# Hybrid block on Trainium2: the linear recurrence of the last two token blocks moved beside the attention's heads 5 to 7, with buffers of its own

## The chip, the cores and the metric

One Trainium2 chip, one core of it. The metric is the device time of one execution in microseconds (us); the time of a kernel is the median of its runs.

## What is computed

One layer of a hybrid encoder, f32, width 1024, on 2048 tokens with 16 learned meta tokens ahead of them (T = 2064). A normalised input goes through one projection `w_in`, whose columns are shared out among three groups of heads that do not depend on each other:

```
p = rms_norm(h, norm_mix_pre) @ w_in          # split by columns into the three groups
y = concat(rg_lru_group, forgetting_attention_group, rwkv7_group)
h = h + rms_norm(y @ w_out, norm_mix_post)
h = h + rms_norm(ffn(rms_norm(h, norm_ffn_pre)), norm_ffn_post)   # conv-gated, 2816 wide
```

The group that the change moves is the gated linear recurrence (LRU) of 256 channels:

```
u = causal_dwconv(xa, conv_w) + conv_b                  # 4 taps
r, i = sigmoid(u @ ga_w + ga_b), sigmoid(u @ gx_w + gx_b)   # 4 heads of 64x64
log_a = -8 * r * softplus(-lam);  a = exp(log_a)
b = sqrt(-expm1(2 * log_a)) * (i * u)
h_t = a_t * h_(t-1) + b_t                               # scan over the tokens
out = h * gelu(ya)
```

The attention has 8 heads of 64, causal, with a decay per token added to the scores; RWKV-7 has 4 heads of 64 with a 64x64 state that runs through the tokens.

## The kernel before

**Stages.** The input projection comes in three parts (matmuls at L193 to L195). Beside it, and on into the next stage, runs the generator `recurrences(part)`: token blocks 0 to 2, 3 to 5 and 6 to 8 (block 0 has 208 tokens, blocks 1 to 7 have 256, block 8 has 64). For each block it runs the RWKV part up to a point called SOLVED, then `R.ending`, which is what is left of the RWKV part of the block before, and then `lru_block` for the block. After the loop the rest of `R.ending` (block 8's own) is run out, the recurrences' pools are closed, and the attention follows in the program. Then come `w_out`, the feed-forward up and down products, each in three matmuls of split operands, and the output.

**Order.** Each engine executes its own instructions strictly in order. That order is not the program's: the kernel is written with generators and then laid out by a scheduler, which lets the attention's first heads run in among the last recurrences. `tc.issue_after(x)` keeps what is in it from being placed ahead of x. SyncE (SP) issues nearly all DMAs, also in order.

**The LRU** (`lru_block`, L1529 to L1591) works on two halves of 128 channels, so four chunks for blocks 7 and 8. One chunk loads its input (L1549), makes the convolution `rwlu` (ScalarE L1556, three VectorE L1558), two gate matmuls into one PSUM bank `eps` (L1563, L1564), reads that bank with ScalarE and VectorE (L1565 to L1567), goes through ScalarE and VectorE by turns (L1568 to L1580, with a square root at L1579, which loads another activation table), scans (L1581), keeps the last column as state `lru_h` (L1582), makes the gelu of the second input in `rwlr` (L1585 to L1589, a tanh at L1588), multiplies (L1590) and stores to `scr_mix` (L1591). `R.t` gives its SBUF buffers (`rwlu` two deep), `R.pe` its bank.

**RWKV closing chain.** The last pieces of a block: small matmuls into `rps` (L1316 to L1472), each read by VectorE or ScalarE before the next can go; a normalisation in VectorE on `rwgsm` and `rwxu` (L1453 to L1461, with a Newton square root at L79 to L84), and the output gate (L1472 to L1480).

**Attention** (`Attn.run`). Half 0 takes query blocks 0 and 1 of all 8 heads, half 1 query blocks 2 and 3. For each head and block `maxima` makes score tiles (L644) in the two-deep PSUM ring `at.mx`, VectorE reduces each to a maximum `mc` (L649), and four transposes (L659, the same ring) make a shift of it. Two steps (AHEAD) later `weights` makes the scores again (`sc`, L773 and L774), ScalarE's exponential (L778), sums on VectorE or GpSimd (L817), and the product with the values (`po`, L796); 14 such products for each head in half 0. `tick` is called within this and on every second call advances a generator `beside`, which is empty in half 0 and works on the 16 meta tokens in half 1. At the start of half 1 `rear` prepares a third buffer for keys, `k2_2`: its fixed rows are cast from the identity (L566), its pool taken before half 0.

Of the kernel before, what the change touches and what calls it, by code (L numbers as in the profile page):

```python
# [1 line left out]

# [6 lines left out]
F32 = mybir.dt.float32  # L9
# [9 lines left out]
P = 128  # L19
# [491 lines left out]
class Attn:  # L511
# [63 lines left out]
    def t(self, shape, tag, dt=F32, bufs=2):  # L575
        return self.pool.tile(shape, dt, tag=tag, name=self.core.n(tag), bufs=bufs)
# [335 lines left out]
    def run(self, pool, third):  # L912


        self.queue = self.nc.sync
        ready = []
        for half, bs in enumerate(((0, 1), (2, 3))):
            if half:
                self.rear(third, "k2_2")
                self.beside = self.meta(pool)  # L920
            for h in range(NH):
                self.wide = (half, h) >= WIDE
                with self.core.tc.issue_after(self.core.settled) if not half and h < 2 else nullcontext():
                    keys = self.keys(h, 4 * bs[-1] + 5)
                for b in bs:
                    gen, total, out = self.maxima(h, b, keys), self.pieces(b), []

                    def fill(share, gen=gen, total=total, out=out):
                        while len(out) < min(total, share * total):
                            out.append(next(gen))  # L930

                    if len(ready) == self.AHEAD:
                        self.weights(*ready.pop(0), fill)
                    fill(1.0)
                    ready.append((h, b, keys, next(gen)))
                    self.serial += 1
                    self.later.append((self.clock + self.FINISH, self.serial, lambda gen=gen: next(gen, None)))
                    self.later.sort(key=lambda x: x[:2])
                    if len(ready) < self.AHEAD + 1 and not half and h == 0:
                        next(gen)  # L940
        self.tail = True
        for i, step in enumerate(ready):
            if i == len(ready) - 1:
                self.queue = self.nc.gpsimd
            self.weights(*step, lambda share: None)
        self.flush()
        for _ in self.beside:
            pass
        while len(self.later) > 1:
            self.later.pop(0)[2]()  # L950
# [644 lines left out]

class Banks:


# [554 lines left out]
PACE = 1.25  # L2155

WIDE = (0, 5)

LATE, NORMS = 8, 2

# [35 lines left out]
def recurrences(core, R, lk, f_bias, scr, blocks, part):  # L2196


    for blk in blocks:
        gate_block(core, R, f_bias, scr, blk[2])  # L2200
        yield
    for b in ((0, 1, 2), (3, 4, 5), (6, 7, 8))[part]:
        gen = R.block(b)
        while next(gen) != R.SOLVED:
            yield
        yield from R.ending
        R.ending = gen
        yield from lru_block(core, R, scr, lk, b)


_INS = [
# [9 lines left out]
def hybrid_block_kernel(ctx: ExitStack, tc: tile.TileContext, args, out):  # L2221
    a = {s: v[0] if s != "meta_tokens" else v for s, v in args.items()}
    nc = tc.nc
    core = Core(tc, ctx)
    scr = scratch(tc, ctx, core)
# [8 lines left out]
    def pool(es, name, bufs, **kw):  # L2234
        return es.enter_context(tc.tile_pool(name=name, bufs=bufs, **kw))

    right = {"side": "right"}
# [9 lines left out]
    with ExitStack() as p1:  # L2247
# [2 lines left out]
        rec = ExitStack()  # L2250
        ps_rw = pool(rec, "ps_rw", 2, space=PSUM, **right)
        ps_ae = pool(rec, "ps_ae", 1, space=PSUM, **right)
        rc = pool(rec, "rc", 1, **right)
        gp = pool(rec, "gp", 1, **right)
        rp = pool(rec, "rp", 1, **right)
        with ExitStack() as p1a:
            ps_mm = pool(p1a, "ps_mm", 5, space=PSUM)
            pools = {"x1": pool(p1a, "x1", 1)}
            gpre = pool(p1a, "gpre", 1)
            pools["us"], pools["rp"] = pool(p1a, "us", 1), rp  # L2260
            pools |= {"nt": pool(p1a, "nt", 4), "w": pool(p1a, "w", 2), "st": pool(p1a, "st", 2)}
            two = p1a.enter_context(ExitStack())
            pools["xn"] = pool(two, "xn", 1, **right)
            sums = up_sums(core, pools["us"], a["ffn_up"], scr, EARLY)
            split_out = w_out_split(core, pools["nt"], a["w_out"], scr)
            core.power = core.const.tile([P, 1], F32, name="power")
            nc.vector.memset(core.power[:], -0.5)
            core.held = [token_load(core, pools, meta, META), token_load(core, pools, x[:P, :], P)]
            g_pre = spread(gpre, a["norm_mix_pre"], "g_pre")
            following = w_in_norm(core, pools, ps_mm, x, meta, g_pre, 0)  # L2270
            for part in range(3):
                blocks = following
                units = w_in_part(core, pools, ps_mm, a["w_in"], blocks, scr, part)
                for i in range(READY if part == 0 else 0):
                    while not next(units):
                        pass
                    if i == 4:
                        core.begun = core.loaded.ins
                if part == 0:
                    zeros = pools["st"].tile([P, PAD], F32, tag="sth", name="zeros")  # L2280
                    nc.vector.memset(zeros[:], 0.0)
                    for r in range(0, A_ROWS + C_ROWS, P):
                        with tc.issue_after(core.powered.ins):
                            nc.gpsimd.dma_start(scr["p"][r : r + P, 0:PAD], zeros[:])
                    with tc.issue_after(core.powered.ins):
                        attn_consts(core)
                    shared, core.const = core.const, rc
                    p1c = ExitStack()
                    p1c.enter_context(tc.issue_after(core.begun))
                    p1c.enter_context(tc.issue_after(core.powered.ins))  # L2290
                    rk = rwkv_consts(
                        core, gp, ps_ae,
                        {
                            s[5:]: (v.rearrange("h d -> (h d)") if s == "rwkv_r_k" else v)
                            for s, v in a.items() if s.startswith("rwkv_")
                        },
                    )
                    lk = lru_consts(
                        core, gp, ps_ae,
                        {  # L2300
                            "conv_w": a["lru_conv_w"], "conv_b": a["lru_conv_b"], "ga_w": a["lru_gate_a_w"],
                            "ga_b": a["lru_gate_a_b"], "gx_w": a["lru_gate_x_w"], "gx_b": a["lru_gate_x_b"],
                            "lam": a["lru_lambda"],
                        },
                    )
                    core.const = shared
                    columns(core, gp, ps_ae, [a["ffn_conv"].rearrange("i (r p) -> (i r) p", p=P)], "", cw)
                    p1c.close()
                    R = Rwkv(core, rp, dp, ps_rw, ps_ae, scr, rk)
                    beside = Beside(PACE)  # L2310
                i = READY + 1 if part == 0 else 1
                for whole in units:
                    if whole and i == READY + 1:
                        beside.add(recurrences(core, R, lk, a["fox_f_bias"], scr, blocks, part))
                    beside.advance()
                    if not whole:
                        continue
                    if part == 1 and i > 1:
                        next(split_out, None)
                    if part and i % 2 == 0:  # L2320
                        with tc.issue_after(core.loaded.ins):
                            next(sums, None)
                    i += 1
                    if part == 2 and i == SETTLED:
                        core.settled, core.parted = core.loaded.ins, core.split.ins
                run(sums) if part == 2 else None
                if part == 1:
                    two.close()
                    pools["xn"] = pool(p1a, "xn2", 1, **right, **early)
                if part < 2:  # L2330
                    following = w_in_norm(core, pools, ps_mm, x, meta, g_pre, part + 1)
                else:
                    core.power = None
# [6 lines left out]
        with ExitStack() as p1b:  # L2340
# [5 lines left out]
                at = Attn(core, ap, ps_at, more, scr, front)  # L2346
            at.second = pool(p1b, "ap2", 1, **early)

            pool(p1b, "pad", 1, **right).tile([P, 23872], F32, name="pad")
            at.run(pool(p1b, "mt", 1, **right, **early), pool(p1b, "k2", 1, **right, **early))  # L2350
    qp = pool(ctx, "qp", 1, **early)
    gf = pool(ctx, "gf", 1, **early)
    with ExitStack() as p3:
# [183 lines left out]
```

## Time and profile before

| | us |
|---|---|
| runs | 2953.79, 2942.76, 2957.45 |
| median of the runs | 2953.79 |
| the profiled execution's own time | 2948.27 |
| its span | 2946.6 |
| instructions | 53222 |
| mean granted TensorE clock | 0.98 |

The profiled execution is 5.52 us below the median and within the runs; the 1.67 us between its time and its span lie outside the instructions. PE is TensorE, PEld its weight loads, DVE VectorE, ACT ScalarE, POOL GpSimd, SP SyncE. In the views by stretch a row gives start:end, length, busy time and instructions of each engine, the granted clock of TensorE (PEclk, 1.00 is full), the share of the DMA engines that was busy, and GB/s. In the groups a row gives the number of instructions, their busy time, the mean of one in ns, and the engine's idle time ahead of them with its cause. In the chain of waits a row gives start, length and what it was.

The LRU of blocks 7 and 8 runs between 870 and 981 us, the whole of half 0's attention up to about 1117 us. The stretch in which recurrences and attention run side by side, 846 to 1062 us, is the one that the change touches first.

### The profile page before, as it was taken

To read this page: it belongs to the slowest core of one execution; us is meant where nothing else is said; L and a number is where in the kernel's file an instruction comes from. 1 tells how busy PE (TensorE), PEld (TensorE's weight loads), DVE (VectorE), ACT (ScalarE), POOL (GpSimd) and SP (SyncE) were. 2 spreads that over 40 slices of the span, in tenths; PEclk is the share of its full clock that TensorE was granted. 3 is DMA by queue.
4 is the path that set the end of the run, shared out by engine and by line. 5 is a ranking of instruction groups with operands and counts; after the bars stand their busy time and mean duration, and the time that the engine had idled before them with its cause. 6 is when DMAs were issued, how large, how long until landed. Compare 5 with 4: busy or idle time off the path is not lost.

```text
span 2946.6 us, 53222 instructions
## 1 busy us (share of the span) xinstructions
PE 2832.0 (96%) x18854; PEld 2441.3 (83%) x18854; DVE 1997.5 (68%) x3839; ACT 1504.0 (51%) x2937; POOL 1302.6 (44%) x1572
## 2 busy tenths in 40 slices
PE   8999999989988889999999999999999999999998
PEld 8998989978965555666578999999999999787887
DVE  4357654665678665556656988888787787656766
ACT  3246442554446554555645666666666665324333
POOL 1002221222114567667624666456655444656443
PEclk9999999999989899999999999999999999999999
DMA  7775678577643357445264665577767764436453
GB/s 244 250 243 190 220 232 289 181 234 244 204 122 79 79 130 222 100 121 128 49 192 148 210 195 179 157 231 210 220 200 223 215 198 148 141 112 218 151 171 122
DMA packets 470344, 530.51 MB, mean 180 GB/s; under 512 B 86863, under 2 KB 356889, under 8 KB 468525
## 3 DMA queue, kind: packets, MB, share of 16 engines
q1 hardware_dynamic: 469308, 526.18, 59.1%
q8 instruction: 148, 2.42, 0.4%
q0 software_dynamic: 768, 0.93, 0.1%
q14 instruction: 120, 0.98, 0.1%
HBM read 368.07 MB, written 158.90 MB: 179 GB/s over the span
## 4 chain that ended last, share of the span: by engine, by line
PE 69%; DVE 8%; DMA 5%; ACT 5%; issue 2%; POOL 2%; SPq 1%; DVEq 0%; POOLq 0%; ACTq 0%
PE psu L193 10%; PE psu L194 9%; PE psu L195 9%; PE psd L193 4%; PE psd L194 4%; PE psd L195 4%; PE po L796 4%; PE psp L193 2%; PE psp L195 2%; PE psp L194 2%; PE mx L644 2%; PE sc L773 2%; PE pswo L193 2%; PE pswo L194 2%; PE pswo L195 2%
## 5 line engine op out<-in xcount | busy, mean ns | idle before, releaser
L194 PE MATMUL psu<-xo,uw 128*128 128x344 f32 x1848 | 592.0, 321 | 0.0
L193 PE MATMUL psu<-xo,uw 128*128 128x344 f32 x1848 | 586.6, 322 | 3.3 <-DVE vb L1971 2.2
L195 PE MATMUL psu<-xo,uw 128*128 128x344 f32 x1848 | 582.4, 320 | 0.6 <-DVE uw L1780 0.6
L193 PE MATMUL psp<-xh,wh 128*128 128x384 f32 (+2 forms) x1152 | 379.9, 330 | 0.7 <-DMA wh<-scr_wk 0.7
L194 PE MATMUL psp<-xl,wh 128*128 128x384 f32 (+2 forms) x1152 | 374.8, 325 | 0.0
L195 PE MATMUL psp<-xh,wl 128*128 128x384 f32 (+2 forms) x1152 | 373.2, 324 | 0.0
L1780 DVE TENSOR_TENSOR uw<-uq,uw 128x512 fp32r<-128x512 f32 x341 | 313.6, 924 | 61.6 <-ACT uw L1779 58.1
L193 PEld LDWEIGHTS psu<-xo,uw 128*128 128x128 f32 x1848 | 346.1, 188 | 4.7 <-DVE vb L1971 2.7
L194 PEld LDWEIGHTS psu<-xo,uw 128*128 128x128 f32 x1848 | 347.4, 188 | 0.0
L195 PEld LDWEIGHTS psu<-xo,uw 128*128 128x128 f32 x1848 | 346.0, 188 | 1.4 <-DVE uw L1780 1.4
L1779 ACT ACTIVATE uw<-uq 128x512 fp32r<-128x512 f32 x462 | 287.8, 627 | 104.8 <-PE psu L195 46.0
L778 ACT ACTIVATE p<-sc,bias 128x512 f32<-128x512 f32 (+4 forms) x352 | 197.3, 590 | 161.6 <-PE sc L774 138.0
L649 DVE TENSOR_REDUCE mc<-mx 128x1 f32<-128x512 f32 (+5 forms) x352 | 191.6, 566 | 113.8 <-PE mx L644 81.0
L1919 DVE SCALAR_TENSOR_TENSOR uy<-psu,ffn_cols,uy 128x342 f32<-128x342 f32 (+1 forms) x390 | 220.8, 567 | 64.6 <-ACT uy L1917 62.2
L1927 POOL TENSOR_TENSOR uy<-uy,uy 128x342 f32<-128x342 f32 (+1 forms) x132 | 146.9, 1113 | 229.5 <-DVE uy L1919 69.3
L1780 POOL TENSOR_TENSOR uw<-uq,uw 128x512 fp32r<-128x512 f32 x121 | 184.8, 1527 | 132.6 <-ACT uw L1779 113.2
L193 PEld LDWEIGHTS psp<-xh,wh 128*128 128x128 f32 x1152 | 218.2, 189 | 6.5 <-issue 3.4
L194 PEld LDWEIGHTS psp<-xl,wh 128*128 128x128 f32 x1152 | 218.4, 190 | 5.5 <-issue 4.0
L195 PEld LDWEIGHTS psp<-xh,wl 128*128 128x128 f32 x1152 | 218.2, 189 | 4.4 <-issue 3.1
L817 POOL TENSOR_TENSOR acc<-acc,p 128x512 f32<-128x512 f32 (+3 forms) x186 | 197.0, 1062 | 47.4 <-DVE acc L817 22.6
L1780 DVE TENSOR_TENSOR fo<-u,fo 128x896 fp32r<-128x896 f32 x88 | 101.2, 1150 | 131.7 <-ACT fo L1779 131.2
L1779 ACT ACTIVATE fo<-u 128x896 fp32r<-128x896 f32 x88 | 81.2, 923 | 209.2 <-PE psd L195 112.9
(492 smaller groups left out, 6288.3 us busy)
## 6 DMA issues: line engine op xcount, KB each, us to landing
uq<-scr_us SPq DMA_DIRECT2D x220, 256.0 KB
uq<-in_ffn_up_dram SPq DMA_DIRECT2D x209, 256.0 KB
wl<-scr_wk SPq DMA_DIRECT2D x48, 512.0 KB
wh<-scr_wk SPq DMA_DIRECT2D x48, 512.0 KB
u<-scr_ff SPq DMA_DIRECT2D x88, 256.0 KB
scr_ff<-uy SPq DMA_DIRECT2D x110, 171.0 KB
raw<-in_w_in_dram SPq DMA_DIRECT2D x24, 512.0 KB
scr_wk<-wh SPq DMA_DIRECT2D x24, 512.0 KB
```

The costliest lines, as they stand in the source:

```text
L193: nc.tensor.matmul(out, ah, bh, start=first, stop=False, skip_group_check=more)
L194: nc.tensor.matmul(out, ah, bl, start=False, stop=False, skip_group_check=more)
L195: nc.tensor.matmul(out, al, bh, start=False, stop=last, skip_group_check=more)
L644: nc.tensor.matmul(ps[:rows, : e - a], q3[:, qo : qo + rows], k2[:, a:e], start=True, stop=not last)
L649: self.reduced = nc.vector.tensor_reduce(mc[:rows, i, ci : ci + 1], ps[:rows, : e - a], axis=AX.X, op=ALU.max)
L778: last = nc.scalar.activation(p[:rows, :w], ps[:rows, :w], AF.Exp, bias=bias[:rows, j : j + 1])
L796: mm = nc.tensor.matmul(po[at : at + 64, c0:n], v1[:rows, j], p[:rows, : n - c0], start=start and i < 2, stop=end and i + 2 >= len(group), ...
L817: eng.tensor_tensor(a, ps_[0][0][:rows, c0:n] if start and i == 1 else a, p[:rows, : n - c0], op=ALU.add)
L1779: core.nc.scalar.activation(hi, src, AF.Copy)
L1780: (eng or core.nc.vector).tensor_tensor(lo, src, hi, op=ALU.subtract)
L1919: core.conved = stt(y[:, :n], src[:, i : n + i], cw[:, 44 * i + cc : 44 * i + cc + 1], y[:, :n], op0=ALU.mult, op1=ALU.add)
L1927: core.pooled = nc.gpsimd.tensor_tensor(v[:, :n], g[:, :n], v[:, :n], op=ALU.mult)
```

## The change

`recurrences` no longer runs `lru_block` for blocks 7 and 8 (LAST). Their two generators are chained into `at.rest`. At half 0, head 5 (RESUME), `Attn.run` makes this chain the `beside` generator, so that every second tick advances it; what is left of it when half 0 ends is run out before half 1. For this the LRU gets buffers that outlive the recurrences' pools: a pool `lr` of its own with `rwlu` three deep instead of two, its constants in a pool `lc`, and for the gate matmuls the attention's own ring `at.mx` in place of `eps`. The filler `pad` shrinks by the same 536 floats for each partition. The pool of the third key buffer is taken only after `lr` has been closed, so it may lie where `lr` lay. The instructions are the same in number and shape; lines that stand behind the change are numbered one or five higher (L644 becomes L645, L1316 becomes L1321, L1563 becomes L1568).

```diff
+                for _ in self.rest:
+                    pass
-                self.rear(third, "k2_2")
+                self.rear(third(), "k2_2")
                 self.beside = self.meta(pool)
             for h in range(NH):
+                if (half, h) == RESUME:
+                    self.beside = self.rest
...
+class Spare:
+    def __init__(self, core, pool, at):
+        self.core, self.pool, self.pe = core, pool, at.mx
+    def t(self, shape, tag, bufs=1):
+        return self.pool.tile(shape, F32, tag=tag, name=self.core.n("rw" + tag), bufs=3 if tag == "lu" else bufs)
...
+LAST, RESUME = (7, 8), (0, 5)
...
-        yield from lru_block(core, R, scr, lk, b)
+        if b not in LAST:
+            yield from lru_block(core, R, scr, lk, b)
...
+        lc = pool(p1, "lc", 1, **right)
...
+                    core.const = lc
...
-            pool(p1b, "pad", 1, **right).tile([P, 23872], F32, name="pad")
-            at.run(pool(p1b, "mt", 1, **right, **early), pool(p1b, "k2", 1, **right, **early))
+            pool(p1b, "pad", 1, **right).tile([P, 23872 - 536], F32, name="pad")
+            mt = pool(p1b, "mt", 1, **right, **early)
+            early_half = p1b.enter_context(ExitStack())
+            spare = Spare(core, pool(early_half, "lr", 1, **right, **early), at)
+            at.rest = chain(*(lru_block(core, spare, scr, lk, b) for b in LAST))
+
+            def third():
+                early_half.close()
+                return pool(p1b, "k2", 1, **right, **early)
+
+            at.run(mt, third)
```

**What moves in the engines' order.** On PE the gate matmuls of the four chunks stand behind 0, 5, 28 and 33 value products of the attention in the kernel before, and behind 56, 56, 70 and 75 in the changed one. The last RWKV matmul stands behind 84 value products before and behind 56 after. Up to 50 value products the two kernels have the same RWKV work behind them, but for one matmul.

First place, PE, the start of block 8's closing chain (`rps`, `rwxu`, `rwxf`, `rww`, `rwsc`: RWKV; `mx`, `sc`: attention). Before:

```order
L1316 MATMUL rps_11105<-rwxu_11062,rwsc_10594 32x32 x3
L644 MATMUL mx_12463<-k_1402_11222,q_1403_11227 128x512 [waits Activation_49]
L646 LDWEIGHTS identb
L646 MATMUL mx_12463<-futureb,identb 128x128
L644 MATMUL mx_12479<-k_1402_11222,q_1403_11227 128x400 [waits Activation_49]
L644 MATMUL mx_12482<-k_1402_11222,q_1403_11227 128x512 [waits DVE_49]
L1316 MATMUL rps_11112<-rwxf_11073,rwxu_11062 32x32 [waits DVE_49] x2
L1316 MATMUL rps_11112<-rwxf_11073,rwxu_11062 32x32 x2
L1360 MATMUL rps_11119<-rww_1335_10595,rwsc_10594 64x64 [waits PE_49]
L1360 MATMUL rps_11119<-rww_1335_10595,rwsc_10594 64x64 x3
L773 MATMUL sc_12497<-q_1666_12147,k_1409_11245 128x272 [waits Activation_49]
```

The same steps in the changed kernel:

```order
L1321 MATMUL rps_10956<-rwxu_10913,rwsc_10521 32x32 x3
L1321 MATMUL rps_10963<-rwxf_10924,rwxu_10913 32x32 [waits DVE_49] x2
L1321 MATMUL rps_10963<-rwxf_10924,rwxu_10913 32x32 x2
L1365 MATMUL rps_10970<-rww_1321_10522,rwsc_10521 64x64 [waits PE_49]
L1365 MATMUL rps_10970<-rww_1321_10522,rwsc_10521 64x64 x3
L1376 MATMUL rps_10978<-rww_1321_10522,rwxf_10924 64x128 [waits Activation_49] x2
L1376 MATMUL rps_10978<-rww_1321_10522,rwxf_10924 64x128 x2
L1397 MATMUL rps_10988<-rwsc_10521,rwxu_10977 64x128 [waits DVE_49]
L1397 MATMUL rps_10988<-rwsc_10521,rwxu_10977 64x128 x3
L1409 MATMUL rps_10996<-rww_1321_10522,rwsc_10521 64x64 [waits PE_49,Activation_49]
```

The attention's score tiles that stood between the chain's steps are gone; the chain's 40 rows stand on PE one behind the other, and its 34 rows on VectorE too.

Second place, PE, the end of the same chain in the changed kernel, and what follows it:

```order
L1473 MATMUL rps_11045<-ident,rwxu_11006 128x64 [waits Activation_49]
L1477 MATMUL rps_11047<-rwsg_10433,g_up 128x64 [waits DVE_49]
L1568 MATMUL mx_12152<-rwlu_12144,lru_ga_w 128x256 [waits DVE_49]
L1569 MATMUL mx_12152<-rwlu_12144,lru_gx_w 128x256
L645 MATMUL mx_12185<-k_1374_11073,q_1377_11086 128x272
```

The first LRU chunk comes straight behind the chain, and the attention's next score tile, which takes its place in the ring `mx` after the LRU's tile, behind both.

Third place, VectorE, the end of half 0, with the casts into the third key buffer (`k_1917`). Before:

```order
L860 RECIPROCAL dcol_12704<-dcol_12704 16x32 [waits DMAHW2_49]
L649 TENSOR_REDUCE mc_12887<-mx_12950 128x1 [waits PE_49]
L649 TENSOR_REDUCE mc_12887<-mx_12892 128x1 [waits PE_49]
L649 TENSOR_REDUCE mc_12887<-mx_12969 128x1 [waits PE_49]
L566 CAST k_1917_13019<-ident 64x520 x4
L649 TENSOR_REDUCE mc_12887<-mx_12972 128x1 [waits PE_49]
```

And in the changed kernel:

```order
L1595 SCALAR_TENSOR_TENSOR rwlu_12644<-rwlu_12644,rwlr_12645 128x64 [waits DVE_49]
L650 TENSOR_REDUCE mc_12890<-mx_12953 128x1 [waits PE_49]
L638 MEMSET mc_13074 128x20 [waits DVE_49]
L650 TENSOR_REDUCE mc_12890<-mx_12895 128x1 [waits PE_49]
L650 TENSOR_REDUCE mc_12890<-mx_12899 128x1 [waits PE_49]
L650 TENSOR_REDUCE mc_12890<-mx_12975 128x1 [waits PE_49]
L567 CAST k_1917_13026<-ident 64x520 [waits DMAHW2_49,DMAHW1_49,DVE_49]
L567 CAST k_1917_13026<-ident 64x520 x3
```

The last step of the LRU (L1595) now stands six rows ahead of the casts, and the first cast waits for DMAs, among them the LRU's last stores, since it writes where `rwlu` lay; before, it waited for nothing.

More of the change, by code (lines that the diff above doesn't have):

```diff
@@ L1 @@
 from contextlib import ExitStack, nullcontext
+from itertools import chain
 import concourse.bass as bass
```

## The prediction

> **What bounds the kernel now.** I read the page's busy times first.
>
> ```profile
> PE 2832.0 (96%) x18854; PEld 2441.3 (83%) x18854; DVE 1997.5 (68%) x3839; ACT 1504.0 (51%) x2937; POOL 1302.6 (44%) x1572
> ```
>
> TensorE is busy for 96% of the span. A change that moves other engines' work can only win time in which TensorE waits for it: 2946.6 - 2832.0 = 114.6 us in all. So I looked next at the stretches from where attention and recurrences start to run side by side to the end of half 0.
>
> ```profile
> 846.00:880.00 34.00, 27.21 (x205) 19.59 (x203) 26.08 (x72) 11.00 (x25) 4.10 (x11) 0.70 0.81 193
> 880.00:915.00 35.00, 26.24 (x365) 17.59 (x365) 29.80 (x76) 28.49 (x65) 20.70 (x37) 0.90 0.33 77
> 915.00:950.00 35.00, 32.12 (x297) 22.17 (x295) 30.28 (x90) 17.77 (x41) 15.37 (x26) 0.90 0.28 70
> 950.00:985.00 35.00, 27.12 (x373) 18.50 (x373) 25.50 (x73) 24.49 (x56) 16.72 (x29) 0.83 0.32 79
> 985.00:1020.00 35.00, 29.72 (x292) 20.39 (x288) 24.59 (x69) 16.07 (x34) 23.43 (x38) 0.94 0.27 67
> 1020.00:1062.00 42.00, 41.74 (x309) 26.33 (x307) 31.11 (x97) 27.66 (x59) 26.71 (x39) 0.95 0.48 116
> 1062.00:1090.00 28.00, 21.13 (x95) 11.73 (x94) 15.49 (x37) 12.85 (x27) 20.70 (x33) 0.93 0.71 134
> ```
>
> From 846 to 1020 TensorE is idle for 6.8 + 8.8 + 2.9 + 7.9 + 5.3 = 31.7 us. The two stretches that hold most of the LRU, 880 to 915 and 950 to 985, are the poorest of the three to five in the middle: 75% and 77%, where 915 to 950 has 92%. But 985 to 1020, with no LRU at all, has 85%: something else, the serial RWKV chain, also holds it back. From 1020 to 1062 TensorE has no hole (99%). The waits of TensorE from 846 to 1020 name the cause.
>
> ```profile
> PE mx L644 <- DVE mc L649: 7.5, 6, 3.3
> ...
> PE mx L644 <- DVE lru_h L1582: 2.9, 1, 2.9
> ```
>
> The longest total is a score tile that waits for VectorE to reduce the tile before it (7.5 us), and VectorE is busy 85% of 880 to 915; once a tile waits directly behind an LRU step. So part of the idle time is VectorE's queue, into which the LRU is laid.
>
> **The LRU taken out of the early stretch (term A).** These are groups from 830 to 985 us, the four chunks of blocks 7 and 8.
>
> ```profile
> L1589 DVE SCALAR_TENSOR_TENSOR rwlr<-rwlr,rwlraw 128x256 f32<-128x256 f32 (+1 forms) x4 | 4.8, 1194 | 2.2 <-ACT rwlr L1588 2.2
> ...
> L1563 PE MATMUL eps<-rwlu,lru_ga_w 128*128 128x256 f32 (+1 forms) x8 | 2.2, 359 | 0.0
> ...
> L1564 PE MATMUL eps<-rwlu,lru_gx_w 128*128 128x256 f32 (+1 forms) x8 | 2.0, 327 | 0.0
> ...
> L1556 ACT ACTIVATE rwlu<-rwlraw,lru_cols 128x64 f32<-128x64 f32 (+1 forms) x3 | 1.5, 494 | 7.0 <-DMA scr_mix<-rwlu 7.0
> ...
> L1582 DVE COPY lru_h<-rwlu 128x1 f32<-128x1 f32 x4 | 0.6, 151 | 0.0
> ```
>
> The 14 VectorE groups from L1589 (4.8 us, the costliest) to L1582 (0.6, the cheapest) add up to 28.7 us. ScalarE's L1556 also waits 7.0 us for a store to leave `rwlu`, which the third buffer shortens and which goes from this stretch anyway. On TensorE the LRU is 2.2 + 2.0 = 4.2 us.
>
> What comes off the end is read from TensorE. The two stretches did 26.24 + 27.12 = 53.4 us of its work in 70; without the LRU's matmuls 49.2. At the 92% of 915 to 950 this takes 53.5 us, 16.5 less; at the 85% of 985 to 1020 it takes 57.9, 12 less. If every hole from 846 to 1020 were the LRU's, 31.7 + 4.2 = 36 us would go. Nothing is added to this stretch, so a loss is excluded. I take -16, by the nearest row that keeps the RWKV chain and has little LRU in it. What is late next there is that chain, whose steps stay in their order.
>
> **The closing chain of block 8 (term B).** Between the first and the last of its matmuls that stand in the chain of waits there lie 38 us:
>
> ```profile
> 1024.59 0.26 PE rps L1316 x16
> ...
> 1062.27 0.36 PE rps L1472 x2
> ```
>
> In this time TensorE is 99% busy, since attention stands between the chain's steps; the chain costs nothing but its own matmuls. In the changed order nothing of the attention stands there: 40 TensorE rows and 34 VectorE rows follow one another, so each engine's step is now waited for. Busy time from 1024.4 to 1063 of the instructions that touch `rwgsm` (VectorE only), `rwxu` (PE, PEld, DVE, ACT, POOL) and `rps` (PE, PEld, DVE, ACT):
>
> ```profile
> 1024.40:1063.00 38.60, 6.57 (x19) 1.00 0.51 124
> ...
> 1024.40:1063.00 38.60, 2.67 (x66) 1.71 (x66) 5.28 (x18) 1.23 (x3) 0.00 (x0) 1.00 0.51 124
> ...
> 1024.40:1063.00 38.60, 6.83 (x118) 4.80 (x118) 4.45 (x19) 2.32 (x8) 1.00 0.51 124
> ```
>
> The 6.83 us of matmuls are TensorE's in both kernels. New idle time is VectorE's 6.57 + 5.28 and ScalarE's 1.23: 13.1 us (an instruction that touches both tiles counts twice, the handing over between engines not at all). Lower bound: 6.6, the normalisation alone, in which TensorE has no matmul of the chain to do. Upper bound: the chain takes the 38.6 us that it takes now, less 6.8: +31.8. I take +13, since in the trace the steps wait their turn behind attention's own reductions, which aren't there in the new order.
>
> There is a clock beside it: PEclk is 0.70 from 846 to 880 and 0.83 from 950 to 985, where TensorE idles a fifth of the time, and 0.95 where it has no hole. [...]
>
> **The LRU beside heads 5 to 7 (term C).** Its 4.2 us of matmuls go into a stretch with idle time left: 28 - 21.1 = 6.9 us from 1062 to 1090. VectorE has 42 - 31.1 = 10.9 and 28 - 15.5 = 12.5 us free from 1020 to 1090, 23.4 for its 28.7. So the work nearly fits. What can cost is the order: the gate tile now takes one of the two places in `mx`. How long a tile is held shows ScalarE's timeline, from the read by L1565 to that by L1567:
>
> ```profile
> 875.73 0.47 ACT L1565 ACTIVATE rwlr<-eps,lru_cols 128x256 f32<-128x256 f32 x1 [1.10 <-PE eps L1564]
> ...
> 879.77 0.47 ACT L1567 ACTIVATE rwlg<-eps,lru_rate 128x256 f32<-128x256 f32 x1
> ```
>
> 4.5 us, in which score tiles go through one place instead of two; halved, 2.3 us for each chunk, 9 for four. Queued behind the waiting casts of `k_1917` are VectorE's reductions for half 1's first maxima, and TensorE's next tiles behind these; the store they wait for landed in 4.9 us where the chain of waits shows one, and SP's queue, which the LRU's loads and stores now share with half 1's first loads, is late already by 5.45 us at the turn of the halves:
>
> ```profile
> 721.64 4.89 DMA scr_mix<-rwlu
> ```
>
> ```profile
> 1064.19 5.45 DMA v<-scr_v
> ```
>
> Upper bound: 28.7 - 23.4 = 5.3, and 9, 4.9 and 5.45: +25. Lower bound 0: nothing is taken out of this stretch, which excludes a gain. I take +4, the matmuls at their full price and the rest hidden: six VectorE rows stand between the last LRU step and the casts, and the attention has weights to do (AHEAD) while a score tile waits. If that cover is gone, the 9 of the ring come first.
>
> **Edits at nothing.** The constants in `lc`, the smaller `pad` and the third `rwlu` issue no instruction. The table loads stay as many and move with the square roots, onto a ScalarE with 28 - 12.9 = 15 us free from 1062 to 1090.
>
> **Sum.** -16 + 13 + 4 = +1 against the profiled execution: 2948.3 + 1 = 2949.3. That execution is 5.5 us below the median of the runs; the mean of the four executions shown is 2950.6, and I forecast from that: **2951.6**. A measurement of this kernel can tell about 0.5%, 14.7 us, from no change (the three runs differ by that much).
>
> **Rivals.**
>
> *VectorE was the limit all along (faster).* All holes from 846 to 1020 go: -36 + 13 + 4 = -19, 2931.6. For it: the longest wait is for L649, and VectorE is 85% busy in the worst stretch. Against it: 985 to 1020 has no LRU, VectorE at 70%, and still 5.3 us of holes.
>
> *The bare chain keeps its pace (slower).* Block 8's chain takes its 38 us with nothing beside it: -16 + 31.8 + 4 = +19.8, 2970.4. Its place is the 40 rows behind the attention's 56th value product. For it: the order shows no attention row there on TensorE or VectorE, and at a clock of 0.70 its small steps stretch too. Against it: only about 20 us of the chain (13.1 + 6.83) are work. It decides as soon as the exposed part is over 14.7 + 16 - 4 = 26.7 us.
>
> *The change does nothing to the end.* The early holes are the RWKV chain's own, and what waits there waits as before; the LRU is paid by idle VectorE time here and there: 2950.6. For it: 985 to 1020 again. Against it: the wait behind L1582 and the 7.0 us behind the store are the LRU's own.
>
> **Chances.** Forecast, within 0.5%: 0.43. VectorE the limit: 0.25. Bare chain at its pace: 0.20. Nothing to the end: 0.12. So faster by over 0.5% 0.25, within 0.5% 0.43 + 0.12 = 0.55, slower 0.20. The range reaches down to the first rival with the chain at its lower bound, -36 + 6.6 + 4 = -25.4, 2925; and up to the second with A at 12, -12 + 31.8 + 4 = +23.8, 2974. About 0.08 is left out on either side (C near its upper bound above, holes beyond 1020 that close as well below). The forecast's own range is 2937 to 2965.
>
> **What would show it.** Right: the stretch from 846 to the 56th value product is some 16 us shorter, TensorE at 90% in it; then a piece of about 20 us in which the chain of waits goes from `rps` to `rwgsm` and `rwxu` by turns with TensorE busy for a third of it; then LRU rows beside heads 5 to 7 with TensorE's waits for `mx` little longer than before. Term A is wrong if the early stretch keeps its 82% with no LRU in it. Term B is wrong if TensorE shows no hole at the chain, or one of 30 us. Term C is wrong if score tiles wait for LRU steps by more than some 5 us in all, or if the casts of `k_1917` wait for `scr_mix` stores and TensorE waits behind them. The whole is wrong if the time moves outside this stage, where no instruction has moved.

## The result, and the profile after

The changed kernel takes 2986.53 us (median of 6 runs), the kernel before 2951.34 (median of 6). One of the latter six took 4872.87 us and is left out of the ratio, which is of fast runs alone. This ratio is 1.0122, with a 95% interval of 1.0106 to 1.0139. The changed kernel is slower by about 36 us. The forecast was 2951.6, the range reached to 2974, so the sign and the size were both missed. The profiled execution took 2986.90 us, with a span of 2985.2 against 2946.6: 38.6 us more, which the following lines find.

The page's busy times of the changed kernel:

```profile
PE 2847.1 (95%) x18854; PEld 2444.4 (82%) x18854; DVE 2001.0 (67%) x3839; ACT 1506.0 (50%) x2937; POOL 1303.9 (44%) x1572
```

The work is the same, to 4 us on VectorE and 15 on TensorE. So time was lost waiting. The same stretches as before the change:

```profile
846.00:880.00 34.00, 23.25 (x199) 17.09 (x199) 27.42 (x74) 11.95 (x30) 4.92 (x12) 0.79 0.82 185
880.00:915.00 35.00, 34.04 (x503) 23.79 (x501) 27.51 (x89) 21.10 (x51) 19.45 (x39) 0.96 0.32 75
915.00:950.00 35.00, 29.45 (x206) 18.62 (x205) 24.54 (x66) 18.85 (x40) 17.86 (x26) 0.90 0.32 86
950.00:985.00 35.00, 28.64 (x453) 19.82 (x452) 18.05 (x53) 14.98 (x34) 24.67 (x42) 0.90 0.37 90
985.00:1020.00 35.00, 26.13 (x223) 16.46 (x223) 20.23 (x59) 12.22 (x29) 15.22 (x25) 0.75 0.31 74
1020.00:1062.00 42.00, 27.44 (x119) 16.31 (x116) 23.37 (x62) 20.39 (x42) 10.47 (x13) 0.64 0.21 44
1062.00:1090.00 28.00, 21.47 (x90) 12.33 (x89) 22.20 (x59) 20.89 (x47) 15.37 (x23) 0.77 0.27 69
```

From 880 to 915 TensorE went from 26.24 to 34.04 us: the early relief is there. From 1020 to 1062 it went from 41.74 to 27.44: there the time is lost. Stretches of equal length do not hold equal work, though, so four marks were taken from the timeline of TensorE: the value products (L796, now L797) come in an order that did not change, 14 to a head, two records to a product. Each row below is the start of a group of such records. Before: the last of head 3, the first of head 4, the last of head 5, the last of half 0.

```profile
1012.33 1.74 PE L796 MATMUL po<-p,v 128*64 128x512 f32 x10
...
1026.20 1.74 PE L796 MATMUL po<-p,v 128*64 128x512 f32 x10
...
1060.52 1.74 PE L796 MATMUL po<-p,v 128*64 128x512 f32 x10
...
1115.03 2.48 PE L796 MATMUL po<-p,v 128*64 128x512 f32 x10
```

And after:

```profile
1005.97 1.74 PE L797 MATMUL po<-p,v 128*64 128x512 f32 x10
...
1046.01 1.74 PE L797 MATMUL po<-p,v 128*64 128x512 f32 x10
...
1096.99 2.46 PE L797 MATMUL po<-p,v 128*64 128x512 f32 x10
...
1143.70 1.74 PE L797 MATMUL po<-p,v 128*64 128x512 f32 x10
```

The changed kernel stands at -6.4, +19.8, +36.5 and +28.7 us at these marks, and at +38.6 at the end of the span. So in these two executions 6.4 are won up to the end of head 3; 26.2 are lost between heads 3 and 4 (a gap of 40.0 in place of 13.9); 16.7 in heads 4 and 5; 7.8 come back in heads 6 and 7; and 9.9 are lost in what follows. Such a mark is that of one execution: the profiles of runs 2, 3, 4, 6, 8 and 9 below, whose TensorE has the same records up to there but for one or two, put the 56th product between 995.3 and 1013.9 us (1007.4 here, 1013.8 before). The 6.4 is thus uncertain by several us; the gap of 40, three times the old one, is not.

What lies in the gap of 40 us is read from TensorE's timeline.

```profile
1029.80 0.69 PE L1477 MATMUL rps<-rwsg,g_up 128*128 128x64 f32 x2 [0.17 <-DVE rwxu L1485]
1035.67 1.22 PE L1568 MATMUL mx<-rwlu,lru_ga_w 128*128 128x256 f32 x2 [5.18 <-DVE rwlu L1563]
```

It is first block 7's end, up to 1013.2, then block 8's closing chain up to 1030.6 with no attention in it, then the first LRU chunks. In windows, the chain and what follows it up to the next value product:

```profile
1013.20:1030.60 17.40, 10.48 (x102) 7.93 (x102) 7.89 (x38) 2.74 (x9) 0.00 (x0) 0.50 0.07 19
1030.60:1046.00 15.40, 9.24 (x33) 5.92 (x33) 7.47 (x21) 6.73 (x12) 0.00 (x0) 0.59 0.36 69
```

The chain takes 17.4 us, at a granted clock of 0.50, and the second window 15.4. GpSimd does nothing in either. SP's queue shows one part of the second: the rows from the store that ends block 7 to the LRU's first loads.

```profile
1013.24 0.39 SPq L1487 DMA_DIRECT2D scr_mix<-rww  x1
1013.72 0.41 SPq L614 DMA_DIRECT2D v<-scr_v  x1
1030.77 0.36 SPq L1487 DMA_DIRECT2D scr_mix<-rwxu  x1
1031.18 0.93 SPq L1554 DMA_DIRECT2D rwlraw<-scr_p  x2
```

SP stands for 16.6 us at the store of block 8's result, which waits for the end of the chain, and the LRU's loads stand behind it. GpSimd waits still longer, for a reciprocal of the attention on its way through memory (the waits from 1007 to 1048, SP's and GpSimd's):

```profile
SPq L1487 <- DVE rwxu L1485: 16.6, 1, 16.6
```

```profile
POOL o L867 <- DMA rb<-scr_rden: 34.9, 1, 34.9
```

GpSimd's wait is not the queue's: the reciprocal itself (L861) is made at 1041.5 us, on VectorE behind the chain and the first LRU steps. After the store come a load (2.25 us in the chain of waits), the convolution (5.18 of waiting on TensorE, load included), the gates, and behind them in the ring the attention's score tile. How much of the 15.4 us is the late load's, run 4 tells.

### The profile page after: what moved, and what is told of

Same layout as the page of the kernel before. It is cut to its first block, busy times and chain, and to the rows that moved or that the text cites. A ratio compares the mean times of both kernels' runs of the same rounds, so it can differ in the third digit from the quotient of the medians.

```text
span 2985.2 us, 53221 instructions
## 1 busy us (share of the span) xinstructions
PE 2847.1 (95%) x18854; PEld 2444.4 (82%) x18854; DVE 2001.0 (67%) x3839; ACT 1506.0 (50%) x2937; POOL 1303.9 (44%) x1572
## 4 chain that ended last, share of the span: by engine, by line
PE 73%; DVE 7%; DMA 6%; ACT 5%; POOL 4%; issue 3%; SPq 1%; DVEq 0%; POOLq 0%; ACTq 0%
PE psu L194 9%; PE psu L195 9%; PE psu L196 9%; PE psp L194 4%; PE psp L195 4%; PE psp L196 4%; PE psd L194 4%; PE psd L195 4%; PE psd L196 4%; PE po L797 3%; PE pswo L194 2%; PE pswo L196 2%; PE pswo L195 2%; PE sc L774 2%; PE mx L645 1%
## 5 line engine op out<-in xcount | busy, mean ns | idle before, releaser
L1794 DVE TENSOR_TENSOR uw<-uq,uw 128x512 fp32r<-128x512 f32 x341 | 324.4, 956 | 58.3 <-ACT uw L1793 56.1
L650 DVE TENSOR_REDUCE mc<-mx 128x1 f32<-128x512 f32 (+6 forms) x352 | 191.5, 566 | 111.1 <-PE mx L645 72.7
L1941 POOL TENSOR_TENSOR uy<-uy,uy 128x342 f32<-128x342 f32 (+1 forms) x132 | 143.9, 1090 | 233.5 <-DVE uy L1933 60.7
```

Of the source, the lines that this page charges most:

```text
L650: self.reduced = nc.vector.tensor_reduce(mc[:rows, i, ci : ci + 1], ps[:rows, : e - a], axis=AX.X, op=ALU.max)
L1794: (eng or core.nc.vector).tensor_tensor(lo, src, hi, op=ALU.subtract)
L1941: core.pooled = nc.gpsimd.tensor_tensor(v[:, :n], g[:, :n], v[:, :n], op=ALU.mult)
```

## The experiments

Two theories stood at the start. **P**: the loss is one of order. The LRU's buffers are a new pool on memory of the recurrences' closed pool, so its first step comes behind the last RWKV step; its gate tile has its place in the attention's ring by then, so the attention stops until RWKV has run out, bare. **R**: a gate tile in the ring and the LRU's steps beside heads 5 to 7 cost by themselves, wherever they come from. Ratios are to the kernel before, on the same chip.

**1. The old buffers.** The pool of the recurrences (`rec`, without its banks) is closed at half 1 and not before the attention, and the LRU takes its tiles there. The second weight pool, the third key buffer and the meta tokens' tiles then come at half 1 as well, and `rwlu` is two deep again.

```diff
-        ps_rw = pool(rec, "ps_rw", 2, space=PSUM, **right)
+        ps_rw = pool(banks, "ps_rw", 2, space=PSUM, **right)
...
-        rec.close()
+        banks.close()
...
-            spare = Spare(core, pool(early_half, "lr", 1, **right, **early), at)
+            spare = Spare(core, rp, at)
...
             def third():
-                early_half.close()
+                rec.close()
+                at.second = pool(p1b, "ap2", 1, **early)
```

> The changed kernel, but the recurrences' buffer pool stays open until half 0 is over, and blocks 7 and 8 of the LRU take their tiles there, in the places they had before; the banks are still the attention's ring. The order then has no bare chain: RWKV ends behind 84 value products, the LRU chunks stand behind 56, 61, 70 and 75. Theory P (the pool): what costs is that tiles of a new pool on a closed pool's memory come only behind the last RWKV step, so that the gate tile holds the ring while the chain runs bare; with the old buffers 26 us at the 56th product and the late start of the loads go, and the time is 2935 to 2960. Rival R (the ring and the company): a gate tile in the attention's ring and the LRU's VectorE steps beside heads 5 to 7 cost by themselves; the time stays at 2970 or more.

2943.9 us, 0.998 (0.9967 to 0.9994): as P has it, and R falls as the cause of the whole loss. The gap between heads 3 and 4 is 12.6 us in place of 40.0:

```profile
986.91 1.74 PE L797 MATMUL po<-p,v 128*64 128x512 f32 x10
...
999.48 1.69 PE L797 MATMUL po<-p,v 128*64 128x512 f32 x9
...
1053.85 3.14 PE L797 MATMUL po<-p,v 128*64 128x512 f32 x10
```

But from the first product of head 4 to the last of head 5 it takes 54.4 us, and the kernel before 34.3. What was won early is given back there, so that much of R holds: beside these heads the LRU is not free.

**2. The price of the LRU.** The kernel before, without the LRU of blocks 7 and 8 (their output is a copy of projection rows).

```diff
-        yield from lru_block(core, R, scr, lk, b)
+        if b not in (7, 8):
+            yield from lru_block(core, R, scr, lk, b)
+        else:
...
+            core.nc.sync.dma_start(scr["mix"][0:256, t0 : t0 + n], scr["p"][0:256, PAD + t0 : PAD + t0 + n])
...
```

> The kernel before, with the LRU of blocks 7 and 8 left out (a plain copy of the projection's rows goes to their place). It prices what there is to win from the move. By the term of the prediction 16 us go: 2935. If VectorE was the limit of the early stretch, 30 or more: below 2920. If the RWKV chain sets that stretch, as the times at the 50th value product say (6 us ahead after the change), 4 to 10: 2941 to 2947.

2927.13 us, 0.9928 (0.9909 to 0.9947): 20.4 us less. The two blocks' LRU does cost 20 us where it was, a little more than the 16 of the prediction and much less than all holes. From head 4's first product to head 5's last this kernel takes 37.4 us, against 54.4 with the LRU there in run 1: beside those heads it costs 17. (In both the RWKV part ends behind the 84th product.)

```profile
1000.92 1.74 PE L796 MATMUL po<-p,v 128*64 128x512 f32 x10
...
1038.27 1.97 PE L796 MATMUL po<-p,v 128*64 128x512 f32 x10
```

**3. A later place.**

```diff
-LAST, RESUME = (7, 8), (0, 5)
+LAST, RESUME = (7, 8), (0, 7)
```

> The changed kernel with the LRU taken up at head 7 in place of head 5. The order puts the whole closing chain among heads 4 to 6 again (last RWKV step behind 84 products), and the first LRU chunk right behind it. Theory P: the bare chain goes, the LRU's late loads are still waited for with its tile in the ring: 2950 to 2968. Rival R: the LRU costs as much beside head 7 as beside head 5: 2975 or more.

2981.57 us, 1.0128 (1.0104 to 1.0153). The number is the one that R gave, and P's was missed. But the trace does not show what R says: the closing chain was covered again, as the order has it, and the loss came back as two waits of another kind. TensorE's waits from 1040 to 1130:

```profile
PE mx L645 <- DMA k<-scr_kh: 16.9, 1, 16.9
PE mx L1568 <- DVE rwlu L1563: 14.5, 2, 10.9
```

The gates wait 14.5 us for their input, and a score tile waits 16.9 for the keys in the third key buffer, which lies where the LRU's tiles lay and can only be had when the LRU has ended. From 1090 to 1110 TensorE is all but still:

```profile
1090.00:1110.00 20.00, 1.12 (x4) 0.93 (x4) 9.11 (x36) 10.86 (x24) 1.40 (x2) 0.56 0.23 66
```

So a late LRU is bare at its own end. This is the wait on reuse for which term C had 4.9 us, and it is 16.9 here; at head 5 it did not show.

**4. The loads on GpSimd's queue.**

```diff
-        nc.sync.dma_start(t, scr["p"][row : row + P, a : c0 + n])
+        getattr(R, "queue", nc.sync).dma_start(t, scr["p"][row : row + P, a : c0 + n])
```

(`Spare` sets `queue` to `nc.gpsimd`.)

> The changed kernel with the loads of blocks 7 and 8 of the LRU issued from GpSimd's queue, not from SP's, where they stand behind the store that ends the closing chain. The order keeps the bare chain of 40 TensorE rows. Theory P with the late loads as a part of the loss: data is there when the chain ends, 5 to 10 us go: 2975 to 2982. If the loads are not waited for in earnest (the conv steps stand behind the chain on ScalarE and VectorE anyway), it stays at 2984 to 2989.

2978.98 us, 1.0101 (1.0076 to 1.0126): in the middle of the first forecast, and by the ratios some 6 us faster than the changed kernel. The intervals overlap, so the times do not settle it. The trace says more. The loads are issued long before the chain ends at 1037.3:

```profile
1018.14 1.19 POOL L1554 DMA_DIRECT2D rwlraw<-scr_p  x2
```

ScalarE still makes the convolution only at 1036.70, behind its steps of the chain, but it no longer waits for a load (3.39 us in the changed kernel), and TensorE's wait for it falls from 5.18 to 1.75 us:

```profile
1038.97 1.22 PE L1568 MATMUL mx<-rwlu,lru_ga_w 128*128 128x256 f32 x2 [1.75 <-DVE rwlu L1563]
```

From the end of the chain to the next value product it is still 12.8 us, against 15.4. So the late loads are about 3 us there, and the order is the rest.

**5. Block 8 alone.**

```diff
-LAST, RESUME = (7, 8), (0, 5)
+LAST, RESUME = (8,), (0, 5)
```

> The changed kernel with only block 8 of the LRU (64 tokens) moved beside head 5; block 7 stays where it was before. The order keeps the bare chain of 40 TensorE rows and the late loads behind it, with three quarters of the LRU's work back in the early stretch. Theory P (the bare chain and what hangs on it are most of the loss): 2965 to 2985. Theory W (the loss is the LRU's own work beside heads 5 to 7, some 17 to 20 us for two blocks in the first set of runs): a quarter of it, and no more than 2960.

2981.63 us, 1.0113 (1.0089 to 1.0137). Block 7, 256 of the 320 tokens, is back in its old place, and the loss is nearly all still there, with the same gap, 38.9 us:

```profile
1014.25 1.74 PE L797 MATMUL po<-p,v 128*64 128x512 f32 x10
...
1053.19 1.74 PE L797 MATMUL po<-p,v 128*64 128x512 f32 x10
```

What is lost there does not depend on how much LRU is moved, only on that some of it is.

**6 and 7. Half 1, and its control.** The LRU ahead of the meta tokens in half 1, in a pool of its own; for its room `NP, MORE = 9, 5` becomes `9, 2`. The control is the kernel before with this last line alone.

```diff
-                self.rear(third(), "k2_2")
-                self.beside = self.meta(pool)
+                self.rear(third, "k2_2")
+                self.beside = chain(self.rest, self.meta(pool))
...
```

> The changed kernel with the LRU of blocks 7 and 8 taken up only at the start of half 1, ahead of the meta tokens, from a pool of its own below the third key buffer; for its room the attention's second weight pool shrinks from 5 to 2 tiles. RWKV has ended before (behind 84 products; the LRU stands behind 93 to 125). If the LRU costs its 20 us wherever it runs, as in the kernel before and beside heads 5 to 7: 2943 to 2955. If it hides where VectorE has idle time beside a full TensorE (half 1 shows VectorE 57 to 62% and TensorE 97 to 99% busy): 2930 to 2940.

> The kernel before with the attention's second weight pool shrunk from 5 to 2 tiles, the control for the run above. No theory of the change speaks of it; half 1 may wait more for ScalarE's exponentials: 2947 to 2960.

2961.95 us, 1.0057 (1.0035 to 1.0079), and the control 2959.63, 1.0046 (1.0029 to 1.0063). Both forecasts of run 6 were missed upward, and the smaller weight pool alone explains most of that. Against its control the move wins nothing: the hope that half 1 hides the LRU failed. The order takes it up behind 93 products already, at the turn of the halves, so whether the middle of half 1 would hide it is not tried.

**8. A new pool on the old place.** The changed kernel with its pool laid, by fillers, on the bytes where the recurrences kept the LRU's buffers, with `rwlu` two deep as there, and with a third key buffer that waits for nothing of it.

```diff
-            pool(p1b, "pad", 1, **right).tile([P, 23872 - 536], F32, name="pad")
+            pool(p1b, "pad", 1, **right).tile([P, 5440], F32, name="pad")
+            spare = Spare(core, pool(p1b, "lr", 1, **right, **early), at)
+            pool(p1b, "pad2", 1, **right).tile([P, 16088], F32, name="pad2")
...
```

> The changed kernel with its new pool laid, by two fillers, exactly where the recurrences kept the LRU's buffers; these bytes are last used by block 6. The third key buffer is a pool of its own again and waits for no LRU store. The order is that of the changed kernel, bare chain included. If it matters that the pool is a new one on a closed one's memory, and not which bytes it takes: 2980 to 2992, as the changed kernel. If the bytes matter (a tile that the closing chain still reads) or the third key buffer's wait does: below 2970.

2984.89 us, 1.0129 (1.0100 to 1.0158): as slow as the changed kernel. These are the bytes of run 1, and the third key buffer is out of it; what differs from run 1 is that the pool is a new one, opened after the recurrences' pool is closed (and that run 1 takes three other pools only at half 1).

**9. Another bank.** Run 8, with the gate products in a bank of the output projection.

```diff
-        self.core, self.pool, self.pe = core, pool, at.mx
+        self.core, self.pool, self.bank = core, pool, bank
...
+    def pe(self):
+        return self.bank.tile([P, 512], F32, tag="wo", name=self.core.n("pswo"), bufs=2)
```

> As the kernel with the new pool laid on the LRU's old place, but the gate products go into a bank of the output projection, not into the attention's ring. The pool is still a new one, so the LRU still comes behind the whole of RWKV, but no tile of the ring waits for it: the order covers the closing chain again (RWKV ends behind 84 products) and the LRU stands behind 93, 93, 103 and 112, at the end of half 0. Theory P (the held ring tile turns the late pool into a bare chain): the 33 us at the 57th product go; the LRU ends half 0 with less beside it: 2945 to 2965. If the new pool costs without the ring too: 2975 or more.

2960.66 us, 1.0054 (1.0033 to 1.0075). The pool is a new one still, and the LRU still comes behind all of RWKV (93 products). But no tile of the ring waits for it, and the gap between heads 3 and 4 is 6.7 us:

```profile
1007.74 1.74 PE L797 MATMUL po<-p,v 128*64 128x512 f32 x10
...
1014.44 1.74 PE L797 MATMUL po<-p,v 128*64 128x512 f32 x10
```

So it takes both: a late pool, and its tile in a ring on which others wait. Measured in the same way, the gap is 37.7 to 41.6 us in the four profiles that have both at head 5 (the changed kernel, runs 4, 5 and 8), and 6.7 to 14.5 in the ten others. What is left over the kernel before, 0.5%, is put down to an LRU at the end of half 0, which was not followed further.

**10, 11 and 12. Other places with the old buffers.** Run 1 with `RESUME = (0, 3)`, with `LAST = (8,)`, and with `RESUME = (0, 6)`.

> The run with the old buffers, the LRU taken up at head 3 in place of head 5, so that its chunks stand behind 28 to 47 value products. The runs without the LRU and with the old buffers say that the two blocks cost 17 to 20 us wherever they run. If so: 2940 to 2950. If the RWKV chain leaves room for it around head 3 (at the 42nd product the changed kernel was 28 us ahead of the one before and at the 50th 6, waiting for RWKV): 2930 to 2938.

> The run with the old buffers, only block 8 of the LRU moved beside head 5, block 7 where it was before. If the LRU costs the same in either place, no change: 2943 to 2950. If the small win of the old-buffer run (0.2%) comes from taking block 7 out of the early stretch, none is left; if from block 8, 2940 to 2944.

> The run with the old buffers, taken up at head 6: LRU chunks behind 65, 75, 84 and 89 value products, RWKV's end behind 84. Head 3 cost 0.6% and head 5 won 0.2%. If later is better, since the RWKV chain and the LRU then share less of VectorE: 2935 to 2943. If the LRU then ends too near the turn of the halves, where its buffers have to be closed before the third key buffer and the meta tokens' tiles can be had: 2950 to 2970.

2964.82 us, 1.0058 (1.0040 to 1.0076); 2956.46, 1.0037 (1.0021 to 1.0053); 2949.28, 1.0007 (0.9993 to 1.0020). The first two missed all their forecasts upward, the third lies between its two. No place gives back what the LRU costs; head 5 with both blocks (run 1, faster than the kernel before by 0.2%) is the best that was found.

## Why the prediction was wrong, point by point

**Term A (-16).** What the LRU is worth was about right: without it the kernel before is 20.4 us faster. That moving it would win this in the early stretch was not. By the prediction's own sign (the 56th product some 16 us sooner, TensorE at 90%) the term is wrong, in size: the stretch from 846 to the 56th product is 6.4 us shorter, and TensorE is busy for 83% of it in both kernels. Before:

```profile
846.00:1013.79 167.79, 139.87 (x1512) 96.43 (x1510) 130.28 (x368) 96.58 (x217) 76.38 (x131) 0.86 0.40 95
```

And after:

```profile
846.00:1007.43 161.43, 133.49 (x1485) 90.38 (x1484) 110.94 (x320) 75.07 (x171) 78.71 (x136) 0.87 0.42 100
```

At the 38th product the changed kernel was 28.1 us ahead, but with 382 RWKV records of TensorE still to come where the kernel before had 286; at the 48th both had 126, and the lead was 7.2. Most of the lead was RWKV work put off. "What is late next there is that chain" was said, and not priced.

**Term B (+13).** Right in sign and near in size, but not as it was added up. The chain runs bare in 17.4 us; less the 6.83 of matmuls in the kernel before this is +10.6. TensorE's idle time in it is 17.4 - 10.48 = 6.9 us and not 13.1, and the steps of `rwgsm` and `rwxu` that made up the 13.1 take 4.00 + 4.41 + 1.23 = 9.6. The other 3.7 of the 10.6 are slower matmuls, which the sum did not have, so that the number came so near is in part luck. (The same 19 rows of `rwgsm` took 6.57 us in the kernel before, with GpSimd busy for 26.90 of the 38.6 us, and 4.00 here, where GpSimd is idle; why was not tried.) The rival that has the chain keep its 38 us is wrong, though it had the sign right. The slower matmuls go with a lower clock: the `rps` records of the chain,

```profile
1013.20:1030.60 17.40, 10.48 (x102) 7.93 (x102) 4.48 (x20) 2.32 (x8) 0.50 0.07 19
```

take 10.48 us at a clock of 0.50, where 118 of them took 6.83 at 1.00; eight of one form, 64x128 (L1376, before L1371), have a median of 417 ns against 270. Ahead of the fall of the clock, from 1009.0 to 1012.4 and still at 1.00, TensorE was busy for 1.7 us, and its longest gap was 1.2. The chain is at 0.50 through its whole length, and its matmuls take at least 10.48 - 6.83 = 3.7 us more. The clock is 0.50 even from 1016.4 to 1023.9, where the gaps between the matmuls are 0.4 us at most. Why the clock fell, and why it stayed low, is not shown.

**Term C (+4).** This is the step that failed, in the words "the attention has weights to do (AHEAD) while a score tile waits". It had none left. The scores of one more step were made by 1005.9 us, ahead of the chain, and its value products (the 57th to the 61st) stand behind the scores of the step after. The rows that follow the chain on TensorE in the changed order show it:

```
L645 MATMUL mx_12185<-k_1374_11073,q_1377_11086 128x272
...
L660 MATMUL mx_12202<-ident,sh_12200 1x128 [waits Activation_49]
...
L775 MATMUL sc_12271<-q_1379_11092,k_1374_11073 128x512 [waits Activation_49]
```

The second half of that step's scores (L775) needs the shift that the transposes (L660) make in the same ring, behind the score tile (L645), which is behind the LRU's gate tile. So one held place stops maxima, shift, weights and value products alike: in run 9, with the gate tile elsewhere, the gap was 6.7 us. The bound of 9 us for the ring took it for a ring at half its depth, not for one that stands still. Measured, what term C stood for is 15.4 us between the chain and the next product, plus 16.7 in heads 4 and 5: 32 where 4 was taken and 25 was the upper bound. The sum, +1, missed the 38.6 between the two profiles by 37.6 us; 28 of these are term C's and 10 term A's.

**Within heads 4 and 5** the LRU then costs nearly what leaving it out won: 16.7 us here, 17 in run 1 over run 2, where run 2 won 20.4. VectorE's 23.4 free us of the old profile did not hide it. A lower clock goes with it: 0.80 from 1046 to 1099, after the change, where the kernel before had 1.00 in the same products.

```profile
1046.00:1099.00 53.00, 40.26 (x162) 22.14 (x161) 37.12 (x91) 39.30 (x84) 28.98 (x44) 0.80 0.35 83
```

```profile
1026.20:1062.00 35.80, 35.55 (x270) 22.15 (x269) 26.01 (x78) 24.00 (x53) 25.44 (x38) 1.00 0.48 115
```

**SP's queue** was in the sum only as 5.45 us at the turn of the halves. What showed was the store at the chain's end, which held the queue for 16.6 us and with it the LRU's loads; the prediction looked at the order of PE and VectorE alone. By run 4 this is about 3 of the 15.4 us.

**The casts of the third key buffer** waited for nothing that cost time at head 5, as forecast. At head 7 TensorE waited 16.9 us for this reuse.

**What stays open.** Why the scheduler lets tiles of the new pool come only behind the closed pool's last user is argued from runs 1, 8 and 9, not shown. The 9.9 us that the span loses after half 0 lie outside the stage that the prediction looked at, and were not followed. From the 112th product to the end the other profiles take from 2 us less (run 1) to 17 more (run 10) than the kernel before, so this part may belong to the execution and not to the change.

## What to carry to other kernels

A tile that waits in a ring is a lock on all that takes its place behind it (a gap of 37.7 to 41.6 us here, and 6.7 in run 9 with the tile in another bank): ask of each tile put into a shared ring not how long it is held but what its first writer waits for, and which later steps need a place in the ring to go on. Buffers from memory that another stage still owns are not free when the code says so; here the same work in buffers of the old, still open pool was 1.5% faster than in a new pool on the same bytes (0.998 against 1.0129, with three other pools taken later as well). And work whose removal wins 20 us (run 2) does not win it by moving: price the place it goes to with a run, too.

## What the runs showed of the hardware

A chain of small dependent matmuls between three engines ran at a granted clock of 0.50 over all its 17.4 us, and the clock was 0.59 and 0.80 on average in the 15 and 53 us behind it. The 0.80 is not simply what the chain left behind. From 1043.2 us, with attention on TensorE, the clock was 1.00 again, and from 1053.5 it was 0.50:

```profile
1043.20:1053.30 10.10, 7.34 (x33) 3.62 (x32) 6.56 (x12) 9.46 (x16) 4.22 (x4) 1.00 0.10 29
1053.50:1060.00 6.50, 6.05 (x18) 2.73 (x19) 4.33 (x8) 3.26 (x11) 5.30 (x8) 0.50 0.37 86
```
